# Dilated attention on tokens sorted by t mod 4, with a block's scores in one bank

## The chip, the cores and the metric

The kernel runs on one core of one Trainium2 chip. The metric is the device time of one execution in microseconds, as the median of several. Its engines are TensorE (PE, with PEld for its weight loads), VectorE (DVE), ScalarE (ACT), GpSimd (POOL) and SyncE (SP), which issues the DMAs. SBUF is the core's memory of 128 partitions; PSUM holds matmul results, in banks of 512 fp32 per partition.

## The reference

A trunk of two layers on 256 tokens of 2048 features. Layer A is a Mamba-2 mixer; then one set of keys and values is made from its output; layer B is attention in three groups of (window, dilation), eight heads of 128 features each. Every layer ends in a residual sum and a LayerNorm, and an adaLN (`silu(c) @ w + b`) gives shift, scale and gate.

```python
DIL_PATTERNS = ((128, 1), (512, 4), (2048, 16))

def _dilated_window_attention(q, k, v, window, dilation, slopes):
    """Causal dilated sliding window: query t attends t, t-d, ..., t-window."""
    s = jnp.einsum("brnqhe,brnkhe->brnhqk", qb, kb) * (E ** -0.5)
    ...
    alibi = -slopes[:, None, None] * (delta * dilation).astype(f32)[None]
    s = jnp.where(valid, s + alibi, -jnp.inf)
    ...

def reference(x, c, ...):
    for layer in range(DEPTH):
        shift, scale, gate = _adaln(c, ada_w[layer], ada_b[layer])
        h = x * (1.0 + scale) + shift
        y = _ssd_mixer(h, ...) if layer < N_A_LAYERS else _dilated_mixer(h, k_sh, v_sh, ...)
        x = _layer_norm(DEEPNORM_ALPHA * x + (1.0 + gate) * y, ln_g[layer], ln_b[layer])
        if layer == N_A_LAYERS - 1:
            k_sh, v_sh = _shared_kv(x, kv_w)
    return x
```

The outputs of the three groups are merged by their log-sum-exp, which is one softmax over the keys of all three groups together; a silu gate and the output projection follow. With 256 tokens, every key of a group with dilation d has the same t mod d as its query.

## The kernel before

All weights come from HBM once, in pieces of 128 x 1024 fp32 (512 KB, `raw`, six buffers, SP's queue). The products are made in reduced fp32 (fp32r) from halves: ACT writes the high half of a piece (`whi`, L94) and DVE the remainder (`wlo`, L95), with four buffers of each. PE then multiplies high by high, high by low and low by high (`cm_piece` L119 to L121, `tm_mults` L172 to L174); `cm_wide` (L151, L152) does high against both halves of x in one matmul of 512 columns and low against the high half in one of 256, 16 matmuls per piece.

The adaLN products are made on DVE: `ada_dot` (L236) multiplies a column block of 128 x 2048 (`araw`, 1 MB, two buffers) by the vector `cb_`, which lies in every partition, and sums. 96 such dots are dealt out between the weight pieces as background jobs.

After layer A's LayerNorm, `x_tiles` turns x over, 128 features at a time, 16 tiles: two PE transposes (L711), ACT writes scale times value plus bias as the high half (L714), DVE writes the same in full (`xtmp`, L715) and then the remainder (L716). Their results are the moving operand of the key, value and query projections (`xp`, which holds both halves). These tiles are made between the first pieces of the key projection. At the same time POOL applies the LayerNorm's weight and bias to the residual `u` (L766, L767).

Attention works on one of two query blocks of 128 tokens at a time. For query block b, the keys are those of block 0 to b, so a score matmul (L795) has 128 or 256 columns, three per block, one for each group, each in a PSUM tile of its own. DVE makes a group's bias from a table of distances and one of masks (L797, `bs`, loaded at L773), adds it to the scaled scores (L799), and takes the maximum over all groups (L801); ACT takes exp (L803); DVE normalises (L804, L805). The weights are transposed per group and key block (L809), copied from PSUM by ACT (L815) or, for the second group, DVE (L813), and multiplied with the values (L819, L820). DVE copies the result into `qq` (L821). `attend` does four heads per call and is called twice; after the queries, `z_gate` applies the gate, `split_act` (L195 on ACT, L196 on DVE) makes the halves `oghi` and `oglo`, and the output projection follows.

The order of all of this is not that of the code. A planner (`arrange`) takes the program's instructions, gives each a cost from a table, and, in some rounds of list scheduling, writes one fixed order per engine, which the chip then executes. Matmuls of a following projection are so put between those of attention. An edit at one place can move instructions anywhere.

Of the kernel before, what the change touches and what calls it, by code (L numbers as in the profile page):

```python
# [10 lines left out]
F32 = mybir.dt.float32  # L11
# [3 lines left out]
ALU = mybir.AluOpType  # L15
# [12 lines left out]
H = 8  # L28
# [18 lines left out]
CD, CA, NBIAS = 0, 256, 256 + 768  # L47
# [3 lines left out]
def trunk(ctx, tc, xT, x, c, par, cst, bias, lnrow, ada, wdt, win, wout, wkv, wk1, wbin, wbout, out):  # L51
# [655 lines left out]
    def x_tiles(q):  # L707
        for kt in (2 * q, 2 * q + 1):
            pt = aux.tile([P, 512], F32, name="aux")[:, :L]
            for b in range(2):  # L710
                T.transpose(pt[:, b * P:b * P + P], u[b][:, kt * P:kt * P + P], ident)  # L711
            t = pl.tile([P, L], F32, name="xtmp")
            g_, b_ = pv("lng")[:, kt:kt + 1], pv("lnb")[:, kt:kt + 1]
            S.activation(xhi[:, kt, :], pt, AF.Identity, bias=b_, scale=g_)  # L714
            V.tensor_scalar(t, pt, g_, b_, op0=ALU.mult, op1=ALU.add)  # L715
            V.tensor_tensor(xlo[:, kt, :], t, xhi[:, kt, :].bitcast(F32), op=ALU.subtract)  # L716
# [55 lines left out]
    bs = pc2.tile([P, NBIAS], F32, name="bs", bufs=1)  # L772
    nc.sync.dma_start(bs, bias)  # L773
    dmat = bs[:, CD:CD + 256]
    amask = bs[:, CA:CA + 768].rearrange("p (g k) -> p g k", g=3)
# [9 lines left out]
    def attend(hq, qq):  # L785

        for i in range(4):
            h = 4 * hq + i
            pT = pc2.tile([P, NG, 384], F32, name="pT", bufs=1)
            for b in range(2):  # L790
                n = P * (b + 1)
                sc = pc2.tile([P, NG, n], F32, name=f"sc{b}", bufs=1)
                for g in range(NG):
                    pq = aux.tile([P, 512], F32, name="aux")[:, :n]
                    T.matmul(pq, qq[:, g, i, b * P:b * P + P], kk[hq][:, g, i, :n], start=True, stop=True)  # L795
                    bi = pc2.tile([P, 256], F32, name="bi", bufs=2)[:, :n]
                    V.scalar_tensor_tensor(bi, dmat[:, 256 - n:], SLOPES[g * H + h], amask[:, g, 256 - n:],  # L797
                                           op0=ALU.mult, op1=ALU.add)
                    V.scalar_tensor_tensor(sc[:, g, :], pq, SCALE, bi, op0=ALU.mult, op1=ALU.add)  # L799
                nm = sm.tile([P, 1], F32, name="nm")  # L800
                V.tensor_reduce(nm, sc, axis=AX.XY, op=ALU.max, negate=True)  # L801
# [4 lines left out]
                for g in range(NG):  # L806
                    pp = aux2.tile([P, 512], F32, name="po")[:, :n]
                    for kb in range(b + 1):
                        T.transpose(pp[:, kb * P:kb * P + P], sc[:, g, kb * P:kb * P + P], ident)  # L809

                    d = pT[:, g, 0:P] if b == 0 else pT[:, g, P:384]
                    if g == 1:
                        V.tensor_copy(d, pp)  # L813
                    else:
                        S.activation(d, pp, AF.Copy)  # L815
            po = aux2.tile([P, 512], F32, name="po")[:, :L]
            v = vt[hq]
            for g in range(NG):
                T.matmul(po, v[:, g, 0, i * P:i * P + P], pT[:, g, 0:256], start=g == 0, stop=False)  # L819
                T.matmul(po[:, P:L], v[:, g, 1, i * P:i * P + P], pT[:, g, 256:384], start=False, stop=g == NG - 1)  # L820
# [534 lines left out]
def _layout(x, c, ada_w, ada_b, ln_g, ln_b, a_in_w, a_conv_w, a_conv_b, a_dt_bias,  # L1355
# [25 lines left out]
    delta = 128 + i[:, None] - np.arange(256)[None, :]  # L1381
    bias[:, CD:CD + 256] = -delta
    for g, (win_, dil) in enumerate(((128, 1), (512, 4), (2048, 16))):
        ok = (delta >= 0) & (delta % dil == 0) & (delta <= win_)
        bias[:, CA + 256 * g:CA + 256 * g + 256] = np.where(ok, 0.0, NEG)

# [35 lines left out]
```

## Time and profile before

| | us |
|---|---|
| median of 3 executions | 1284.6 (1283.5 to 1285.86) |
| profiled execution | 1281.55 |
| its span in the trace | 1279.8 |
| mean granted PE clock | 0.993 of full speed |
| x tiles | window 731 to 797 |
| first and second call of attention | windows 1069 to 1112 and 1157 to 1201 |

A row of instructions names its line, engine, operation and tiles, then count, total busy us, mean ns, and idle time of the engine ahead of them with what ended it. The chain of waits is the work that ended last, followed back from the end; its pieces have a start and a length in us. Matmuls are pipelined, so that a matmul's own mean length (393 ns for 512 columns, say) is more than the distance of two of them in the chain. A matmul of two fp32 operands (scores, PV) is recorded as two passes.

### The profile page before, as it was taken

How to read it: one execution, taken by the hardware profiler on the slowest of the kernel's cores; microseconds unless marked ns; L12 is line 12 of the kernel's file. 1: busy time of each engine (PE TensorE's matmuls, PEld its weight loads, DVE VectorE, ACT ScalarE, POOL GpSimd, SP SyncE). 2: the span in 40 equal slices, each digit the busy share in tenths (PEclk: the TensorE clock that was granted, in tenths of full speed). 3: DMA queues.
4: the chain of work that ended last, by engine and by line, in shares of the span. 5: the costliest groups of instructions: out<-in, count | busy, mean ns of one | idle time of the engine just before them, and what ended most of it. 6: DMA issues, size and time to landing. Idle time of an engine off the chain costs nothing.

```text
span 1279.8 us, 19378 instructions
## 1 busy us (share of the span) xinstructions
PE 1239.4 (97%) x7386; PEld 1095.2 (86%) x7386; DVE 1039.2 (81%) x1457; ACT 696.6 (54%) x1027; POOL 33.3 (3%) x20
## 2 busy tenths in 40 slices
PE   6999999999999999999999899999999999999995
PEld 4978999899899999788888699888888888888884
DVE  6999978999998887978895799998745647848778
ACT  4644566868577767764333444444445645444551
POOL 0000000000000000000000135000000000000000
PEclk9999999999999999999999899999999999999998
DMA  9999967887785556578997688999866663453571
GB/s 372 422 422 422 384 216 268 314 276 247 240 300 191 173 159 203 162 258 269 400 376 218 222 315 308 396 420 395 299 191 193 211 185 115 147 183 107 155 266 66
DMA packets 80449, 334.82 MB, mean 262 GB/s; under 512 B 9090, under 2 KB 9314, under 8 KB 67684
## 3 DMA queue, kind: packets, MB, share of 16 engines
q1 hardware_dynamic: 80356, 333.58, 73.5%
q8 instruction: 58, 0.95, 0.3%
q14 instruction: 35, 0.29, 0.1%
HBM read 331.37 MB, written 2.18 MB: 261 GB/s over the span
## 4 chain that ended last, share of the span: by engine, by line
PE 78%; DMA 12%; DVE 7%; ACT 1%; issue 1%; SPq 0%; DVEq 0%; ACTq 0%
PE acc L151 12%; PE acc L174 11%; PE acc L173 11%; PE acc L172 11%; PE acc L152 6%; DMA raw<-in_win 6%; PE acc L119 6%; PE acc L121 6%; PE acc L120 6%; DMA araw<-in_ada 5%; DVE wlo L95 2%; PE py L589 1%; DVE araw L236 1%; PE aux L795 1%; PE po L819 1%
## 5 line engine op out<-in xcount | busy, mean ns | idle before, releaser
L95 DVE TENSOR_TENSOR wlo<-raw,whi 128x1024 fp32r<-128x1024 f32 x395 | 488.9, 1244 | 176.5 <-ACT whi L94 175.2
L94 ACT ACTIVATE whi<-raw 128x1024 fp32r<-128x1024 f32 x395 | 417.1, 1057 | 382.1 <-PE acc L174 178.6
L119 PE MATMUL acc<-actT,whi 128*128 128x256 f32 x960 | 273.6, 288 | 11.8 <-ACT actT L382 7.4
L173 PE MATMUL acc<-wlo,actT 128*128 128x512 f32 x704 | 276.4, 393 | 0.6 <-DVE wlo L95 0.6
L172 PE MATMUL acc<-whi,actT 128*128 128x512 f32 x704 | 274.8, 393 | 1.6 <-ACT whi L94 1.0
L121 PE MATMUL acc<-actT,wlo 128*128 128x256 f32 x960 | 270.5, 285 | 1.4 <-DVE wlo L95 1.4
L120 PE MATMUL acc<-actT,whi 128*128 128x256 f32 x960 | 271.3, 285 | 0.0
L151 PE MATMUL acc<-actT,whi 128*128 128x512 f32 x704 | 251.3, 398 | 0.0
L236 DVE SCALAR_TENSOR_TENSOR araw<-araw,cb__72 128x2048 f32<-128x2048 f32 x96 | 218.4, 2286 | 9.0 <-DMA araw<-in_ada 5.7
L152 PE MATMUL acc<-actT,wlo 128*128 128x256 f32 x704 | 201.8, 287 | 0.6 <-DVE wlo L95 0.6
L119 PEld LDWEIGHTS acc<-actT,whi 128*128 128x128 f32 x960 | 185.2, 194 | 15.7 <-ACT actT L382 9.0
L121 PEld LDWEIGHTS acc<-actT,wlo 128*128 128x128 f32 x960 | 184.0, 193 | 2.3 <-DVE wlo L95 2.0
L120 PEld LDWEIGHTS acc<-actT,whi 128*128 128x128 f32 x960 | 185.1, 193 | 0.3
L174 PE MATMUL acc<-whi,actT 128*128 128x512 f32 x448 | 175.1, 391 | 0.0
L172 PEld LDWEIGHTS acc<-whi,actT 128*128 128x128 f32 x704 | 131.9, 188 | 30.1 <-ACT whi L94 2.8
L151 PEld LDWEIGHTS acc<-actT,whi 128*128 128x128 f32 x704 | 132.2, 188 | 29.2
L173 PEld LDWEIGHTS acc<-wlo,actT 128*128 128x128 f32 x704 | 132.3, 188 | 27.5 <-DVE wlo L95 1.1
L152 PEld LDWEIGHTS acc<-actT,wlo 128*128 128x128 f32 x704 | 133.0, 189 | 1.9 <-DVE wlo L95 1.2
L174 PE MATMUL acc<-whi,ylo 128*128 128x512 f32 x256 | 100.8, 394 | 0.0
L174 PEld LDWEIGHTS acc<-whi,actT 128*128 128x128 f32 x448 | 84.1, 188 | 17.5 <-issue 0.5
L174 PEld LDWEIGHTS acc<-whi,ylo 128*128 128x128 f32 x256 | 48.1, 188 | 9.4
L305 DVE SCALAR_TENSOR_TENSOR cacc<-acc,prm,cacc 128x255 f32<-128x255 f32 (+2 forms) x96 | 43.7, 475 | 2.7 <-ACT cacc L302 2.3
(205 smaller groups left out, 1083.1 us busy)
## 6 DMA issues: line engine op xcount, KB each, us to landing
araw<-in_ada SPq DMA_DIRECT2D x96, 1024.0 KB, 7.2
raw<-in_win SPq DMA_DIRECT2D x160, 512.0 KB, 4.9
raw<-in_wkv SPq DMA_DIRECT2D x72, 512.0 KB, 4.9
raw<-in_wout SPq DMA_DIRECT2D x64, 512.0 KB, 5.6
raw<-in_wbin SPq DMA_DIRECT2D x64, 512.0 KB, 4.0
raw<-in_wk SPq DMA_DIRECT2D x24, 512.0 KB, 6.6
cbc<-cumd SPq DMA_DIRECT2D x16, 512.0 KB, 5.3
raw<-in_wbout SPq DMA_DIRECT2D x16, 512.0 KB, 4.3
```

The costliest lines, as they stand in the source:

```text
L94: S.activation(hi, raw, AF.Copy)
L95: V.tensor_tensor(lo, raw, hi.bitcast(F32), op=ALU.subtract)
L119: T.matmul(o, hi[:, k, c_], ahi[:, kt, :], start=first, stop=False, skip_group_check=True)
L120: T.matmul(o, hi[:, k, c_], alo[:, kt, :], start=False, stop=False, skip_group_check=True)
L121: T.matmul(o, lo[:, k, c_], ahi[:, kt, :], start=False, stop=kt == k1 - 1, skip_group_check=True)
L151: T.matmul(ps[n], hi[:, k, c_], xp[:, kt], start=kt == 0, stop=False, skip_group_check=True)
L152: T.matmul(ps[n][:, 0, :], lo[:, k, c_], xhi[:, kt, :], start=False, stop=kt == KT - 1, skip_group_check=True)
L172: T.matmul(ps[b], h_, hi[:, k, :], start=kt == k0, stop=False)
L173: T.matmul(ps[b], h_, lo[:, k, :], start=False, stop=False)
L174: T.matmul(ps[b], l_, hi[:, k, :], start=False, stop=kt == k1 - 1)
L236: V.scalar_tensor_tensor(raw, raw, 1.0, cb_, op0=ALU.mult, op1=ALU.mult, accum_out=mod[layer][:, ct, j:j + 1])
L305: V.scalar_tensor_tensor(acc[:, o:], ps[:, :L - o], w[:, j:j + 1], acc[:, o:], op0=ALU.mult, op1=ALU.add)
```

## The change

Layer B works on its tokens in the order 0, 4, 8, ..., 1, 5, 9, ..., 2, ..., 3, ... . Block 0 then holds the tokens with t mod 4 of 0 and 1, block 1 the others, and the groups of dilation 4 and 16 need only keys of the query's own block. Dilation 1 needs both blocks, whichever the query block. For each query block there are 128 + 128 + 256 = 512 scores, which fill one PSUM bank.

```diff
             pt = aux.tile([P, 512], F32, name="aux")[:, :L]
             for b in range(2):
                 T.transpose(pt[:, b * P:b * P + P], u[b][:, kt * P:kt * P + P], ident)
+            pt = pt.rearrange("p (j r) -> p r j", r=4)
...
-            S.activation(xhi[:, kt, :], pt, AF.Identity, bias=b_, scale=g_)
-            V.tensor_scalar(t, pt, g_, b_, op0=ALU.mult, op1=ALU.add)
+            S.activation(xhi[:, kt, :].rearrange("p (r j) -> p r j", r=4), pt, AF.Identity, bias=b_, scale=g_)
+            V.tensor_scalar(t.rearrange("p (r j) -> p r j", r=4), pt, g_, b_, op0=ALU.mult, op1=ALU.add)
...
-    bs = pc2.tile([P, NBIAS], F32, name="bs", bufs=1)
+    bs = cb_[:, :NBIAS]
     nc.sync.dma_start(bs, bias)
-    dmat = bs[:, CD:CD + 256]
-    amask = bs[:, CA:CA + 768].rearrange("p (g k) -> p g k", g=3)
+    dmat, amask = bs[:, CD:CD + NKEY], bs[:, CA:CA + NKEY]
...
+            bi = pc2.tile([P, NKEY], F32, name="bi", bufs=2)
+            for g, c in ((1, slice(0, P)), (2, slice(P, 2 * P)), (0, slice(2 * P, NKEY))):
+                V.scalar_tensor_tensor(bi[:, c], dmat[:, c], SLOPES[g * H + h], amask[:, c], op0=ALU.mult, op1=ALU.add)
+            bi = bi.rearrange("p (a k) -> p a k", a=3)
+            pT = pc2.tile([P, 2, 4, P], F32, name="pT", bufs=1)
             for b in range(2):
...
+                cb = slice(b * P, b * P + P)
+                pq = aux.tile([P, 512], F32, name="aux")
+                for g in (1, 2):
+                    T.matmul(pq[:, (g - 1) * P:g * P], qq[:, g, i, cb], kk[hq][:, g, i, cb], start=True, stop=True)
+                T.matmul(pq[:, 2 * P:], qq[:, 0, i, cb], kk[hq][:, 0, i, :], start=True, stop=True)
+                sc = pc2.tile([P, 512], F32, name=f"sc{b}", bufs=1)
+                V.scalar_tensor_tensor(sc.rearrange("p (a k) -> p a k", a=2), pq.rearrange("p (a k) -> p a k", a=2), SCALE,
+                                       bi[:, 0:b + 2:b + 1], op0=ALU.mult, op1=ALU.add)
...
+                pp = aux2.tile([P, 512], F32, name="po")
+                for k in range(4):
+                    T.transpose(pp[:, k * P:k * P + P], sc[:, k * P:k * P + P], ident)
+                if b == 0:
+                    V.tensor_copy(pT[:, b].rearrange("p k q -> p (k q)"), pp)
+                else:
+                    S.activation(pT[:, b].rearrange("p k q -> p (k q)"), pp, AF.Copy)
...
+            T.matmul(po, v[:, 0, 0, ci], pT[:, :, 2, :], start=True, stop=False)
+            T.matmul(po, v[:, 0, 1, ci], pT[:, :, 3, :], start=False, stop=False)
+            for b in range(2):
+                for g in (1, 2):
+                    T.matmul(po[:, b * P:b * P + P], v[:, g, b, ci], pT[:, b, g - 1, :], start=False, stop=b == 1 and g == 2)
             V.tensor_copy(qq[:, 0, i, :], po)
...
-        split_act(oghi[:, c, :], oglo[:, c, :], qs[hq][:, 0])
+        hi, lo = (t[:, c, :].rearrange("p i (j r) -> p i j r", r=4) for t in (oghi, oglo))
+        for i in range(4):
+            split_act(hi[:, i], lo[:, i], qs[hq][:, 0, i].rearrange("p (r j) -> p j r", r=4))
```

The sorting is done where the x tiles are read from PSUM, and undone where the attention output is split. The bias table, of three times 256 columns for distances and the same for masks (768 KB, before 512 KB), lies in `cb_`, the vector that the dots read. The tables themselves are made on the host in the new order. The high and low halves of the attention output are written in the order of the code before. Line numbers after L95 move by one or more: L95, L236, L715 and L716 are L96, L237, L717 and L718; scores are L799 and L800, the scaled add L802, the transposes L812, PV L819, L820 and L823.

The planner writes a new order for the whole program. The first place is DVE in the stretch of the x tiles, some rows in. `wlo` is the low half of a weight piece, `araw` the dot with `cb_`, `xtmp` and `actT` the x tile. Before:

```order
L95 TENSOR_TENSOR wlo<-raw,whi 128x1024
L236 SCALAR_TENSOR_TENSOR araw,mod_83<-araw,cb__72 128x2048
L715 TENSOR_SCALAR xtmp<-aux,prm 128x256 x2
L716 TENSOR_TENSOR actT<-xtmp,actT 128x256
L95 TENSOR_TENSOR wlo<-raw,whi 128x1024
L716 TENSOR_TENSOR actT<-xtmp,actT 128x256
L95 TENSOR_TENSOR wlo<-raw,whi 128x1024
L236 SCALAR_TENSOR_TENSOR araw,mod_83<-araw,cb__72 128x2048
L95 TENSOR_TENSOR wlo<-raw,whi 128x1024
L715 TENSOR_SCALAR xtmp<-aux,prm 128x256 x2
```

and of the changed program, from the same weight split on:

```order
L96 TENSOR_TENSOR wlo<-raw,whi 128x1024
L237 SCALAR_TENSOR_TENSOR araw,mod_83<-araw,cb__72 128x2048
L96 TENSOR_TENSOR wlo<-raw,whi 128x1024
L237 SCALAR_TENSOR_TENSOR araw,mod_83<-araw,cb__72 128x2048
L717 TENSOR_SCALAR xtmp<-aux,prm 128x256 x2
L718 TENSOR_TENSOR actT<-xtmp,actT 128x256
L96 TENSOR_TENSOR wlo<-raw,whi 128x1024
L718 TENSOR_TENSOR actT<-xtmp,actT 128x256
L96 TENSOR_TENSOR wlo<-raw,whi 128x1024 x2
L237 SCALAR_TENSOR_TENSOR araw,mod_83<-araw,cb__72 128x2048
```

A second dot stands ahead of the third pair of x tiles. Up to the last x tile there are ten dots from here on, where there were eight.

The second place is PE in the first call of attention, around the first head's PV. `acc` is the projection that fills, `aux` scores, `po` transposed weights and PV. Before:

```order
L795 MATMUL aux<-kk_7193,qq 128x256
L809 MATMUL po<-cc,sc_10321 128x128 x2
L151 MATMUL acc<-actT,whi 128x512
L152 MATMUL acc<-actT,wlo 128x256
L819 MATMUL po<-pT,vt_7195 128x256
L820 MATMUL po<-pT,vt_7195 128x128
L819 MATMUL po<-pT,vt_7195 128x256
L820 MATMUL po<-pT,vt_7195 128x128
L819 MATMUL po<-pT,vt_7195 128x256
L820 MATMUL po<-pT,vt_7195 128x128
L795 MATMUL aux<-kk_7193,qq 128x256 x2
```

and of the changed program:

```order
L152 MATMUL acc<-actT,whi 128x512
L799 MATMUL aux<-kk_7193,qq 128x128 x2
L819 MATMUL po<-pT,vt_7195 128x256
L820 MATMUL po<-pT,vt_7195 128x256
L823 MATMUL po<-pT,vt_7195 128x128 x4
L800 MATMUL aux<-kk_7193,qq 128x256
L799 MATMUL aux<-kk_7193,qq 128x128 x2
L800 MATMUL aux<-kk_7193,qq 128x256
L153 MATMUL acc<-actT,wlo 128x256
L812 MATMUL po<-cc,sc_10346 128x128 x4
```

The scores of a later head stand around the PV of the first one in both. Between the first score and the last PV of a call PE's order holds 123 and 132 filling matmuls before (first and second call), and 72 and 72 in the changed program. All dots come earlier, as the bias is loaded into `cb_` behind the last of them.

More of the change, by code (lines that the diff above doesn't have):

```diff
@@ L45 @@
 CI, CT, CM, NCONST = 0, 128, 256, 512
-CD, CA, NBIAS = 0, 256, 256 + 768
+NKEY = 768
+CD, CA, NBIAS = 0, NKEY, 2 * NKEY
 @with_exitstack
@@ L1380, in _layout @@
     bias = np.zeros((P, NBIAS), f)
[L1381 to L1385, printed above, removed]
+    at = np.arange(L).reshape(64, 4).T.reshape(-1)
+    delta = at[:, None] - at[None, :]
+    near = delta[:P, :P]
+    delta = np.concatenate([near, near, delta[:P], delta[P:]], 1)
+    win_, dil = (np.repeat(a, (P, P, 2 * L))[None, :] for a in ((512, 2048, 128), (4, 16, 1)))
+    bias[:, CD:CD + NKEY] = -delta
+    bias[:, CA:CA + NKEY] = np.where((delta >= 0) & (delta % dil == 0) & (delta <= win_), 0.0, NEG)
     ada = ada_w.reshape(2, D, 3, KT, P).transpose(0, 2, 3, 4, 1)
```

26 lines of the change are left out of this document (2 added, 24 removed).

## The prediction

> **What bounds the kernel now.** I read three views first: the page's busy times and its chain by engine, then the table of windows, then the chain of waits in the two stretches that the change touches.
>
> ```profile
> span 1279.8 us, 19378 instructions
> PE 1239.4 (97%) x7386; PEld 1095.2 (86%) x7386; DVE 1039.2 (81%) x1457; ACT 696.6 (54%) x1027; POOL 33.3 (3%) x20
> PE 78%; DMA 12%; DVE 7%; ACT 1%; issue 1%; SPq 0%; DVEq 0%; ACTq 0%
> ```
>
> The chain is PE for 78%. But 97% busy is a mean over stages; what the change is worth is settled in the stages where it acts, so the windows come next (columns: length, then busy us and instructions of PE, PEld, DVE, ACT, POOL, then granted clock, DMA share, GB/s).
>
> ```profile
> 0.00:150.00 150.00, 133.78 (x821) 116.88 (x822) 129.58 (x141) 74.69 (x101) 0.20 (x4) 1.00 1.00 410
> ...
> 731.00:797.00 66.00, 65.47 (x542) 65.05 (x542) 65.70 (x65) 28.24 (x35) 33.08 (x16) 0.99 0.85 310
> 830.00:1069.00 239.00, 239.00 (x1196) 202.56 (x1196) 161.70 (x179) 115.80 (x149) 0.00 (x0) 1.00 0.78 267
> 1069.00:1112.00 43.00, 43.00 (x266) 38.43 (x266) 39.42 (x97) 22.15 (x47) 0.00 (x0) 1.00 0.31 94
> 1157.00:1201.00 44.00, 44.00 (x273) 39.22 (x272) 40.10 (x98) 24.18 (x50) 0.00 (x0) 1.00 0.36 109
> 1201.00:1260.00 59.00, 59.00 (x290) 49.76 (x290) 43.29 (x61) 25.45 (x30) 0.00 (x0) 1.00 0.54 187
> ```
>
> The two attention calls are the windows at 1069 and 1157. There PE is never idle, and DVE is at 92% and 91% (39.42 of 43, 40.10 of 44). So in attention a matmul removed is time removed, and a DVE or ACT instruction removed is worth nothing by itself. The window 731 to 797, in which x is turned over into tiles of features by tokens, is the opposite case: DVE 65.70 of 66, with no room at all. Up to 797 PE just keeps pace (65.47), and then the chain of waits passes through DVE:
>
> ```profile
> 792.42 2.25 DVE wlo L95
> 794.72 0.39 PE acc L121
> ```
>
> and PE's own waits between 731 and 830 are few and short:
>
> ```profile
> PE acc L152 <- DVE wlo L95: 0.6, 2, 0.4
> PE acc L121 <- DVE wlo L95: 0.5, 1, 0.5
> ```
>
> So PE and DVE are balanced to within 1.1 us there: the piece of weights that PE needs next arrives from DVE when PE has just run out.
>
> **PE's work in attention.** Scores, transposes and PV as the chain has them (L795 and L819/L820 are recorded as two passes per instruction):
>
> ```profile
> 1157.19 0.44 PE aux L795 x4
> 1157.63 0.23 PE acc L151
> 1159.21 0.12 PE acc L152
> 1159.56 0.43 PE aux L795 x2
> 1165.90 0.44 PE po L809 x4
> 1168.26 0.43 PE po L819 x2
> 1168.69 0.22 PE po L820 x2
> ```
>
> A 128-column score costs 0.44 / 2 = 0.22 us, a 256-column one 0.43, a transpose 0.44 / 4 = 0.11, and PV 0.43 and 0.22 for the same widths. A head had three scores of each width, and has four narrow and two wide: 1.95 becomes 1.74, so -0.21. PV goes from three and three to two wide and four narrow, again -0.21. Transposes go from nine to eight, -0.11. That is -0.53 a head and, over 8 heads, **-4.2 us**. Nothing hides this gain: PE is busy in all 43 and 44 us of both windows, and stays so until 1260. The bounds are -4.2 and, if PE then waits for softmax as often as it is spared work, 0.
>
> **DVE's and ACT's work in attention.** For these I need the costs of one instruction against its length:
>
> ```profile
> L799 DVE SCALAR_TENSOR_TENSOR sc<-aux,bi 128x256 f32<-128x256 f32 x24 | 10.0, 420 | 0.7
> L799 DVE SCALAR_TENSOR_TENSOR sc<-aux,bi 128x128 f32<-128x128 f32 x24 | 6.5, 287 | 2.8 <-PE aux L795 2.0 <-PE po L809 0.6
> L801 DVE TENSOR_REDUCE nm<-sc 128x1 f32<-128x768 f32 x8 | 7.6, 950 | 0.2
> L801 DVE TENSOR_REDUCE nm<-sc 128x1 f32<-128x384 f32 x8 | 4.4, 546 | 0.1
> L805 DVE TENSOR_SCALAR sc<-sc,den 128x768 f32<-128x768 f32 x8 | 4.9, 618 | 0.2
> L805 DVE TENSOR_SCALAR sc<-sc,den 128x384 f32<-128x384 f32 x8 | 3.3, 418 | 0.2
> L803 ACT ACTIVATE sc<-sc,nm 128x768 f32<-128x768 f32 x8 | 7.5, 932 | 3.4 <-DVE nm L801 3.3
> L803 ACT ACTIVATE sc<-sc,nm 128x384 f32<-128x384 f32 x8 | 4.9, 613 | 7.0 <-DVE nm L801 7.0
> L803 ACT ACTIVATION_READ_ACCUMULATOR sc<-sc,nm 128x1 f32 x16 | 3.0, 186 | 0.0
> L804 DVE RECIPROCAL den<-den 128x1 f32<-128x1 f32 x8 | 1.3, 162 | 0.4
> L95 DVE TENSOR_TENSOR wlo<-raw,whi 128x1024 fp32r<-128x1024 f32 x395 | 488.9, 1244 | 176.5 <-ACT whi L94 175.2
> ```
>
> The two L799 rows give 133 ns per 128 columns, so 0.69 us at 512; between the other pairs, 512 columns are 0.68 (maximum), 0.49 (normalise) and 0.72 (exp). Scaled add: 3 x 0.287 + 3 x 0.420 = 2.12 becomes 2 x 0.69 = 1.38. The bias is made once a head instead of per block: 2.12 becomes 0.29 + 0.29 + 0.69 = 1.27. Maximum 1.50 becomes 1.36, normalise 1.04 becomes 0.98, copies of the transposed weights, at L799's prices, 0.71 become 0.69. Together 7.5 become 5.7, -1.8 us of DVE a head, and ACT has less too (one copy of 512 columns in place of four). PE is what ends these windows, so I count **0**. The gain is not kept as slack either, as the order shows: between the first score and the last PV of a call PE's order holds 72 matmuls of the following projection as filling, in both calls, where it held 123 and 132. With PE's 4.36 us of its own a head (1.74 + 1.74 + 8 x 0.11) and 18 fillers, alternately 0.23 and 0.12 us apart, 4.36 + 9 x 0.35 = 7.5 us of PE stand against 7.8 us of DVE rows (the 5.7, 0.42 for PV's copy, 0.3 of reciprocals, and 18/16 of a weight split of 1.24, since 16 fillers use one up). The same sum for before is 7.5 + 0.42 + 0.3 + 2 x 1.24 = 10.7 us, where the window says 39.42 / 4 = 9.9, since neighbouring rows overlap; scaled by that, 7.8 is 7.2, or 96% of PE's time instead of 92%. Bounds: 0 (everything covered) and +1.0 a head, since the second block's way from score to PV is 0.69 + 0.68 + 0.72 + 0.19 + 0.16 + 0.49 + 0.44 + 0.69 = 4.1 plus the first block's 1.86 of DVE, 5.9 us, against a cover of 1.74 + 3.15 = 4.9. The next head's transposes and PV also stand in between, so I am near the lower end: **+0.5** in all.
>
> **The stretch from 731 to 830.** The bias now lies in the buffer that the adaLN dots read, so its DMA cannot go before the last dot, and the order has all dots earlier. In the stretch of the x tiles it has ten dots where it had eight; both orders have had 64 when it starts. DVE's rows there:
>
> ```profile
> L95 DVE TENSOR_TENSOR wlo<-raw,whi 128x1024 fp32r<-128x1024 f32 x20 | 33.1, 1654 | 0.0
> L236 DVE SCALAR_TENSOR_TENSOR araw<-araw,cb__72 128x2048 f32<-128x2048 f32 x8 | 18.2, 2280 | 0.0
> L715 DVE TENSOR_SCALAR xtmp<-aux,prm 128x256 f32<-128x256 f32 x14 | 7.0, 536 | 0.7 <-ACT actT L714 0.6
> ```
>
> The weight splits take 1654 ns in the mean while POOL works (2.25 in the chain above), more than the 1.24 us over the whole run, so DVE cannot make up for anything. Two dots more are 2 x 2.2 = 4.4 us of DVE in a stretch where DVE has 0.3 us free and PE has no reserve, and PE then waits as long. They are missing later, after 830, where DVE is busy 161.70 of 239 us and their absence earns nothing. Of the 4.4 I take off 0.5: the 1.1 us of waits above come partly from this same shortage, and a PE that is late no longer meets them. **+3.9**, bounds 0 (PE lives on splits that were made ahead) and 4.4.
>
> **The x tiles' reads.** ACT's L714 and DVE's L715 now read PSUM with a step of 16 bytes, 16 times each, and write in order. No instruction of the trace reads PSUM with a step. The nearest are additions in SBUF with a step of 12 bytes (x2), against short ones (x16):
>
> ```profile
> L714 ACT ACTIVATE actT<-aux,prm 128x256 fp32r<-128x256 f32 x16 | 8.0, 551 | 0.3 <-PE aux L711 0.3
> L241 DVE TENSOR_TENSOR mod<-mod,adab 128x2 f32<-128x2 f32 x16 | 2.4, 156 | 0.1
> L241 DVE TENSOR_TENSOR mod<-mod,adab 128x16 f32<-128x16 f32 x2 | 0.3, 174 | 0.0
> ```
>
> 14 elements more cost 18 ns, 1.3 ns each, hardly above the 1.04 of L799 (133 / 128): no second cycle. So I take **0**, with +4.3 as the other end (256 x 1.04 ns more for each of the 16 on DVE; ACT's 16 lie in its 38 idle us). [...]
>
> **What is hidden or small.** The last dot and the bias load before:
>
> ```profile
> 914.35 2.29 DVE L236 SCALAR_TENSOR_TENSOR araw<-araw,cb__72 128x2048 f32<-128x2048 f32 x1
> 1006.61 0.33 SPq L773 DMA_DIRECT2D bs<-in_bias  x1
> ```
>
> 92 us lie between the two, so a wait of the bias DMA for the last dot costs nothing, nor do 256 KB more. The attention output is split in 8 pieces of 256 columns instead of 2 of 1024, read with a step of 256 bytes: per four heads, by the slopes above, 0.5 for ACT's first piece and 4 x 0.42 on DVE, 2.2 us, against 1.1 on ACT and then 1.2 on DVE before, so ready no later, and PE is busy throughout 1201 to 1260; **0**, with +1 if the step costs. The order also swaps a few rows and loads in the first 150 us, where DMA is full (share 1.00); there a 1 MB or 512 KB load moved by one place shifts work by at most its own time, 2.6 us at 410 GB/s, either way and mostly back again: I take 0, with -1 to +1.
>
> **Sum** on the profiled execution (1281.55 us for a span of 1279.8): -4.2 + 3.9 + 0.5 = +0.2, so 1281.75. That execution lies 3.05 below the median of 1284.6, so the forecast is **1284.8**.
>
> **The rivals.** B: the two dots cost nothing. For it: only 1.1 us of waits between 731 and 830, and four buffers of splits. Against: DVE without idle time for 66 us. It leaves out the 3.9: 1280.9. C, on the slower side: PSUM with a step goes at half rate, and the full DVE passes it on. It decides as soon as L715's successor is above 0.56 us, since DVE has 0.3 us free for 16 of them; at 0.27 us more each it is +4.3, 1289.1. For it: no reading of PSUM in this trace speaks against it. Against: the SBUF rows. D: with fewer fillers PE waits for softmax. It decides from where a block's way to PV exceeds what stands in between; at half of the 1.0 us a head found above, 8 x 0.5 = 4.0 in place of 0.5, 1288.3. For it: DVE at 96%. Against: the fillers can be prepared early, and PE had no wait there at 92%.
>
> **Chances.** My forecast A 0.50, B 0.23, C 0.13, D 0.14. A difference of 0.2% (2.6 us) is about what a measurement tells from none: faster is below 1282.0, slower above 1287.2. A's own range is 1282 to 1287.5, with its unknowns (±1 at the start, 0 to +1 at the splits, 0 to 4.4 for the dots): faster 0.12, same 0.27, slower 0.11. B: 0.19, 0.04, 0. C: 0, 0.01, 0.12. D: 0, 0.03, 0.11. Together faster 0.31, same 0.35, slower 0.34. The range, 1279.5 to 1290, reaches past B and C by about a microsecond each.
>
> **What would show it.** In the profile of the changed kernel: attention windows shorter by 51 to 60 fillers and by 2.1 us more each, with PE still without idle time (A, B; not D, where PE's waits there name L802 or a copy); between 731 and 830 PE waits for the weight split of some 4 us in place of 1.1 (A) or not (B); the x tiles' DVE row at 0.54 (A, B) or about 0.8 us (C). I would be wrong altogether if the stretch 150 to 731, whose order hardly differs, changed its length, or if PE lost time behind the bias DMA.

## The result, and the profile after

| | before | changed |
|---|---|---|
| median of 20 executions, us | 1285.01 (1283.36 to 1291.98) | 1289.56 (1285.78 to 1292.2) |
| profiled execution, us | 1281.55 | 1289.36 |
| its span, us | 1279.8 | 1287.5 |
| mean granted PE clock | 0.993 | 0.990 |

The ratio is 1.0027, with a 95% interval of [1.0016, 1.0037]: the change costs 2 to 5 us, 3.5 in the middle. The forecast was 1284.8, no difference that can be told, in a range of 1279.5 to 1290. The time lies near the range's upper end and above the 1282 to 1287.5 that the forecast gave for its own mechanism; the sign is that of the slower rivals. One kernel's executions scatter by 6 to 9 us. The two profiled ones are 7.8 us apart, more than the medians, and the one of before, 1281.55, lies below all 20 executions of the table, so a difference of the two traces is too large by some 3 us. Below, the traces tell the mechanism and the ratios the size. Ratios are turned into microseconds with some 1285.5 us for the kernel before.

The page of the changed kernel, busy times and the chain by engine:

```profile
span 1287.5 us, 19278 instructions
PE 1240.0 (96%) x7378; PEld 1093.5 (85%) x7378; DVE 1031.9 (80%) x1399; ACT 694.9 (54%) x1009; POOL 34.0 (3%) x20
PE 76%; DMA 14%; DVE 7%; issue 1%; ACT 1%; SPq 0%; DVEq 0%; ACTq 0%
```

PE is busy as long as before (1240.0 us against 1239.4) in a span 7.7 us longer, so it waits more, and the chain has more DMA. Where, is seen by the start of the same instruction in both. First the changed kernel's timeline of PE (start, length, what, and the idle time ahead with its releaser):

```profile
732.25 0.69 PE L712 MATMUL aux<-cc,u 128*128 128x128 f32 x2 [5.73 <-ACT u L697]
1082.40 0.39 PE L799 MATMUL aux<-kk,qq 128*128 128x128 f32 x2
1229.36 0.40 PE L173 MATMUL acc<-whi,kk 128*128 128x512 f32 x1
```

and the same three of the kernel before, the first x tile, the first score, and the first matmul of the output projection:

```profile
726.73 0.48 PE L711 MATMUL aux<-cc,u 128*128 128x128 f32 x1 [5.73 <-ACT u L696]
1069.66 0.50 PE L795 MATMUL aux<-kk,qq 128*128 128x128 f32 x3
1221.39 0.39 PE L172 MATMUL acc<-whi,kk 128*128 128x512 f32 x1
```

| stretch | before | changed | difference |
|---|---|---|---|
| start to first x tile (layer A) | 726.73 | 732.25 | +5.5 |
| first x tile to first score | 342.93 | 350.15 | +7.2 |
| first score to output projection (attention) | 151.73 | 146.96 | -4.8 |
| output projection to the end of the span | 58.4 | 58.1 | -0.3 |

So in this pair of traces attention gained what it should, the x tiles lost more than the forecast had, and layer A, whose instructions the change doesn't touch, lost 5.5 us. Layer A's waits sit at one place. PE's timeline there, in the changed kernel:

```profile
233.09 0.73 PE L173 MATMUL acc<-whi,actT 128*128 128x512 f32 x2 [2.13 <-ACT whi L95]
234.20 0.66 PE L560 MATMUL aux<-cc,xs 128*128 128x128 f32 x4 [0.37 <-ACT cb L539]
236.25 1.12 PE L590 MATMUL py<-xd,seg 128*128 128x64 f32 x4 [1.40 <-DVE xd L562]
```

and in the kernel before:

```profile
232.84 1.46 PE L589 MATMUL py<-xd,seg 128*128 128x64 f32 x9 [0.46 <-DVE xd L561]
```

PE waits 3.9 us in three pieces where it waited 0.7 (0.46 here and 0.19 at 235.26). The clock falls as well. This is the window 223 to 247 of the kernel before, then of the changed one (the sixth of the plain figures from the left, after POOL, is the granted clock):

```profile
223.00:247.00 24.00, 23.33 (x128) 19.61 (x127) 21.93 (x31) 20.01 (x33) 0.00 (x0) 1.00 0.93 355
```

```profile
223.00:247.00 24.00, 20.10 (x99) 16.36 (x98) 17.82 (x24) 17.82 (x38) 0.00 (x0) 0.86 0.84 323
```

In windows of 0.5 us the clock of the changed kernel is 1.00 from 223 to 235 us and from 242 to 247, and 0.50 between 235.5 and 241.5. The mean of 0.86 over 24 us is then 2 x 0.14 x 24 = 6.7 us at half speed, and PE does 99 matmuls instead of 128. If PE had work for all of this time, that cost up to 3.4 us by estimate; with the 3.2 us of longer waits this is more than the 5.5, so how the loss divides between the two is not settled. What was late is in the chain of waits of the changed kernel, in order of time:

```profile
213.20 7.58 DMA cumd<-araw
220.81 0.33 SPq L544
221.70 7.43 DMA araw<-in_ada
229.26 2.30 DVE araw L237 x2
231.56 0.35 DVE cb L538
232.00 1.23 DVE seg L552
233.23 2.36 DVE cacc L306 x6
235.59 0.61 DVE xd L562
```

`cumd` is a small tensor that goes to HBM and comes back in every partition (`cbc`, L544). SP's new order issues a dot's 1 MB load directly ahead of the write and two weight loads behind it; the write takes 7.58 us, and SP stands on L544 until it has landed. The next dot's load starts only then, and that dot stands in DVE's queue ahead of the products that PE needs. ACT is late by the same write: it waits 5.70 us for `cbc` (0.98 us before), and the high half that PE waits for longest, 2.13 us, is made behind that. ACT's timeline in the changed kernel:

```profile
225.36 3.33 ACT L549 ACTIVATE seg<-cbc,cumT 128x128 f32<-128x128 f32 x11 [5.70 <-DMA cbc<-cumd]
```

Between the x tiles and the first score PE waits for weight splits (waits of PE, 728 to 825 us: in total, times, longest), and DVE's rows in the same window are these:

```profile
PE acc L122 <- DVE wlo L96: 2.9, 4, 1.0
PE acc L153 <- DVE wlo L96: 1.1, 1, 1.1
PE aux L712 <- DVE xtmp L717: 0.9, 1, 0.9
```

```profile
L96 DVE TENSOR_TENSOR wlo<-raw,whi 128x1024 fp32r<-128x1024 f32 x27 | 38.0, 1417 | 0.0
L237 DVE SCALAR_TENSOR_TENSOR araw<-araw,cb__72 128x2048 f32<-128x2048 f32 x14 | 36.2, 2583 | 2.1 <-DMA araw<-in_ada 2.0
L718 DVE TENSOR_TENSOR actT<-xtmp,actT 128x256 fp32r<-128x256 f32 x16 | 10.2, 641 | 0.1
L717 DVE TENSOR_SCALAR xtmp<-aux,prm 128x256 f32<-128x256 f32 x16 | 8.0, 536 | 0.6 <-ACT actT L716 0.6
```

and ACT's row for the same tiles, over the whole run:

```profile
L716 ACT ACTIVATE actT<-aux,prm 128x256 fp32r<-128x256 f32 x16 | 8.1, 554 | 0.7 <-PE aux L712 0.7
```

The waits for splits are 4.0 us where the kernel before had 1.1, and one of 0.9 us for an x tile comes on top. In the same window of the kernel before the dots took 2282 ns and the splits 1508: the dots have become longer and the splits shorter. The stepped reads (L717 with 536 ns against 536, L716 with 554 against 551) cost nothing.

In attention PE has no idle time in either kernel: from the first score to the output projection it is busy 151.73 of 151.73 us before, and 146.96 of 146.96 in the changed kernel. The rows of 512 columns measured what the forecast had read off between the shorter ones:

```profile
L802 DVE SCALAR_TENSOR_TENSOR sc<-aux,bi 128x512 f32<-128x512 f32 x16 | 10.9, 686 | 1.6 <-PE aux L800 1.2 <-PE po L812 0.3
L805 DVE TENSOR_REDUCE nm<-sc 128x1 f32<-128x512 f32 x16 | 10.6, 677 | 0.1
L809 DVE TENSOR_SCALAR sc<-sc,den 128x512 f32<-128x512 f32 x16 | 7.6, 482 | 0.3
L807 ACT ACTIVATE sc<-sc,nm 128x512 f32<-128x512 f32 x16 | 11.4, 715 | 7.5 <-DVE nm L805 7.5
```

(0.69, 0.68, 0.49 and 0.72 us had been worked out.) The split of the attention output, in the changed kernel:

```profile
L196 ACT ACTIVATE kk<-qq 128x256 fp32r<-128x256 f32 x8 | 4.8, 663 | 0.3 <-DVE qq L831 0.3
L197 DVE TENSOR_TENSOR vt<-qq,kk 128x256 fp32r<-128x256 f32 x8 | 4.7, 628 | 0.3 <-ACT kk L196 0.3
```

256 columns should have taken DVE 0.42 us.

### The profile page after: what moved, and what is told of

It is laid out like the page before. It is cut to its first block, busy times and chain, and to the rows that moved or that the text cites. A ratio compares the mean times of both kernels' runs of the same rounds, so it can differ in the third digit from the quotient of the medians.

```text
span 1287.5 us, 19278 instructions
## 1 busy us (share of the span) xinstructions
PE 1240.0 (96%) x7378; PEld 1093.5 (85%) x7378; DVE 1031.9 (80%) x1399; ACT 694.9 (54%) x1009; POOL 34.0 (3%) x20
## 3 DMA queue, kind: packets, MB, share of 16 engines
HBM read 331.63 MB, written 2.18 MB: 259 GB/s over the span
## 4 chain that ended last, share of the span: by engine, by line
PE 76%; DMA 14%; DVE 7%; issue 1%; ACT 1%; SPq 0%; DVEq 0%; ACTq 0%
PE acc L152 12%; PE acc L175 11%; PE acc L174 11%; PE acc L173 11%; PE acc L153 6%; DMA raw<-in_win 6%; DMA araw<-in_ada 6%; PE acc L120 6%; PE acc L122 6%; PE acc L121 6%; PE py L590 2%; DVE wlo L96 2%; DVE araw L237 1%; DMA prm<-in_par 1%; DVE seg L552 1%
## 5 line engine op out<-in xcount | busy, mean ns | idle before, releaser
L96 DVE TENSOR_TENSOR wlo<-raw,whi 128x1024 fp32r<-128x1024 f32 x395 | 485.5, 1236 | 188.7 <-ACT whi L95 186.7
L95 ACT ACTIVATE whi<-raw 128x1024 fp32r<-128x1024 f32 x395 | 417.1, 1057 | 383.1 <-PE acc L175 177.7
L237 DVE SCALAR_TENSOR_TENSOR araw<-araw,cb__72 128x2048 f32<-128x2048 f32 x96 | 222.7, 2329 | 16.5 <-DMA araw<-in_ada 12.8
L549 ACT ACTIVATE seg<-cbc,cumT 128x128 f32<-128x128 f32 x128 | 40.2, 388 | 13.0 <-PE py L590 7.2
```

The lines of the kernel that those rows point to most:

```text
L95: S.activation(hi, raw, AF.Copy)
L96: V.tensor_tensor(lo, raw, hi.bitcast(F32), op=ALU.subtract)
L237: V.scalar_tensor_tensor(raw, raw, 1.0, cb_, op0=ALU.mult, op1=ALU.mult, accum_out=mod[layer][:, ct, j:j + 1])
L549: S.activation(seg[:, hh, b, :], cbc[:, hh, b, :], AF.Relu, bias=cumT[:, b, h0 + hh:h0 + hh + 1], scale=-1.0)
```

## The experiments

All instructions up to the bias load are the same in both programs, and both orders have done the same set of them when the first `xtmp` is made. So one program can be given the other's order for a part. "Layer A" is that common set; "up to the last dot" is what either order has done when its last adaLN dot is made, with the x tiles in it. A list `HEAD` of instruction numbers, written out in the kernel, takes the place of the planner's order:

```diff
+    mine = set(HEAD)
+    best = best[0], HEAD + [i for i in best[1] if i not in mine]
     last = {}
     for i in best[1]:
```

### The changed program, layer A in the order before

> The changed program, but all instructions up to the first xtmp stand in the order of the kernel before (they are the same instructions in both). Theory T: the profiled loss of 5.5 us ahead of the x tiles is the new order's, by the loads and the cumd write on SP near 213 us. Then the first transpose of the x tiles falls back from 732.3 to about 726.7 us, the clock stays whole near 235 us, and the time is 4 to 6 us under the changed kernel's, 1284 to 1286. Rival R: that loss is chance of one execution (a clock that fell), and the order costs nothing. Then the time stays within 1.5 us of the changed kernel's 1289.6.

Measured: 1284.43 us, ratio to before 0.9988 [0.9975, 1.0001]. Against the change's 1.0027 that is 5.0 us less (3 to 7 by the two intervals). The first x tile starts at 726.42 us, and the window 223 to 247 has its full clock again:

```profile
223.00:247.00 24.00, 23.03 (x124) 19.20 (x123) 21.96 (x31) 19.75 (x33) 0.00 (x0) 1.00 0.91 350
```

PE's longest gap there is 0.76 us. The theory holds: the order, not chance, cost layer A its time. The granted clocks of all executions say the same: with the old order of layer A, 106 of 171 had a mean of 0.991 or more, with the changed or a mixed order 1 of 68. Some executions with the old order lose clock too, then; where in them no trace shows.

### The changed program, everything up to the last dot in the order before

> The changed program with everything up to the last adaLN dot in the order of the kernel before; attention, the reads of PSUM with a step and the split of the attention output are those of the change. Theory T: the x tiles lose 7.2 us by the order alone (dots and their loads earlier), and what is left of the change is attention's gain of 4.8 us. Then it takes 4 to 5 us less than the kernel before, about 1280, and PE waits for weight splits between 731 and 830 us for about 1 us. Rival S: the stretch of the x tiles loses by the stepped reads or by something else of the change; then it keeps at least half of the 7.2 us and the time is 1284 or more.

Measured: 1278.68 us, ratio 0.9952 [0.9933, 0.9971], -6.2 us, **faster than both kernels**. From the first x tile to the first score it takes 343.71 us (342.93 before), so the stepped reads and the bias in `cb_` are not what lost time there. PE's waits there:

```profile
PE acc L153 <- DVE wlo L96: 0.9, 2, 0.7
PE acc L122 <- DVE wlo L96: 0.5, 1, 0.5
```

Its attention takes 4.8 us less than that of before in the trace, as in the changed kernel; the ratio's interval (-8.6 to -3.7 us) holds that number.

### The kernel before, layer A in the changed order

> The kernel before, with all instructions up to the first xtmp in the changed program's order, and nothing else of the change. Theory T: it loses what the changed kernel lost there, 4 to 6 us: 1289 to 1291 against 1285, first transpose of the x tiles near 732 us, PE waiting some 2 us for a high half near 231 us. Rival R (chance): within 1.5 us of the kernel before.

Measured: 1290.16 us, ratio 1.0037 [1.0022, 1.0052], +4.8 us. The first x tile starts at 731.88 us, with PE gaps of 0.72, 0.37 and 2.03 us near 232 to 236 and a clock of 0.86 in the window 223 to 247. The long wait fell on the product (L561) and not on a high half, otherwise as expected. Nothing of the change is in this kernel but the order of layer A. Even so its trace loses time behind layer A too: from the first x tile to the first score it takes 346.80 us, +3.9, with the rows of the x tiles, and the eight dots among them, as before. PE's waits there:

```profile
PE acc L121 <- DVE wlo L95: 2.8, 2, 2.4
PE acc L152 <- DVE wlo L95: 0.7, 1, 0.7
```

So one trace of this stretch can be some 4 us longer, with 3.5 us of waits for splits, without any dot moved.

### The kernel before, from the first x tile to the last dot in the changed order

> The kernel before, with the instructions from the first xtmp to the last adaLN dot in the changed program's order, so with ten dots in the stretch of the x tiles in place of eight; the x tiles read PSUM without a step, and attention and the bias tile are as before. Theory T: it loses about 7 us, 1291 to 1293 against 1285. Rival S (the stepped reads or other parts of the change cost it): under 3 us of loss.

Measured: 1289.63 us, ratio 1.0032 [1.002, 1.0044], +4.1 us [2.6, 5.7]; less than expected, and far from nothing. First x tile to first score: 349.10 us in the trace, +6.2. Over all traces without a further edit of the stretch it took 342.9 to 346.8 us with the old order of the x tiles (four kernels) and 349.0 to 351.3 with the changed one (five). Together the three pieces make 4.8 + 4.1 - 6.2 = +2.7 us, against 3.5 [2, 5] measured for the change.

### Layer A again: only the loads around the `cumd` write

Of layer A's changed order, 17 rows of SP go back (rows 116 to 132 of its queue: the `cbc` loads stand right behind the write again, and the dot's load behind them). A second kernel has 16 rows of DVE put back as well.

```diff
+seq["SP"][116:133] = before["SP"][116:133]
+seq["DVE"][178:194] = before["DVE"][178:194]    # the second kernel only
```

> The changed program in its own order, except for 17 rows of SP's queue around the cumd write near 213 us, which stand as in the kernel before: one 1 MB load of araw and two weight loads move from ahead of the cbc loads to behind them. Every other engine keeps the changed order. Theory T1: these rows are the whole loss ahead of the x tiles; then the first transpose is at 726 to 728 us and the time at 1284 to 1286, as with the whole of layer A in the old order. Rival: the order of DVE, ACT or PE in layer A takes part; then the first transpose stays 2 us or more behind 726.7 us.

Measured: 1288.39 us, ratio 1.0012 [0.9997, 1.0027], -1.9 us against the change, which is not clear of the noise; the first x tile starts at 733.47 us. The rival holds. The write is now quick, ACT's wait for `cbc` is 0.42 us, and the wait has moved to a dot, which stands ahead of where its load can be ready. Chain of waits of this kernel, and DVE's timeline:

```profile
213.57 2.18 DMA cumd<-araw
216.63 7.24 DMA araw<-in_ada
```

```profile
223.96 2.29 DVE L237 SCALAR_TENSOR_TENSOR araw<-araw,cb__72 128x2048 f32<-128x2048 f32 x1 [5.87 <-DMA araw<-in_ada]
```

> The changed program in its own order, except for the 17 rows of SP's queue as in the run that brought the cumd write forward, and 16 rows of DVE's queue there, three dots among them, which stand behind a weight split (one also behind the product that the cumd write sends) as in the kernel before. Theory L: the loss ahead of the x tiles is dots that stand in DVE's queue ahead of their loads' landing; the loads alone did not mend it because a dot then waited 5.9 us. With both, DVE's wait for araw there is under 2 us, the first transpose is at 726 to 728.5 us, the time 1283.5 to 1286. Rival: the order of ACT or PE there has a part; then the first transpose stays behind 729 us.

Measured: 1288.93 us, ratio 1.0018 [1.0001, 1.0035]; the first x tile at 732.75 us. DVE's waits for `araw` between 200 and 237 us fell to 4.7 us (8.1 in the changed kernel, 7.2 with the loads alone, 1.1 before), PE's gap is one of 2.59 us, and the clock still falls (0.79 in the window). Neither the theory's number nor its time came. Ahead of the gap its chain of waits still has the write, 4.55 us here, and behind it a dot's load of 10.11 us. The part that these rows have in the loss is not told apart from the others'.

### The x tiles: DVE's time, the loads, or POOL

The first three kernels start from the kernel before with the changed order from the first x tile to the last dot (+4.1 us), the fourth from the changed kernel. In the first, two of the ten dots multiply 64 columns:

```diff
+        n = 64 if dots.append(0) or len(dots) - 1 in (65, 68) else D
+        V.scalar_tensor_tensor(raw[:, :n], raw[:, :n], 1.0, cb_[:, :n], op0=ALU.mult, op1=ALU.mult,
```

> The kernel before with the changed order from the first xtmp to the last dot, whole (ten dots in the stretch of the x tiles), but two of these ten dots multiply 64 columns in place of 2048; their 1 MB loads stay. It leaves out most of the sum in those two. Theory D: the loss of 4 to 6 us comes from DVE's time for the two dots, 2 x 2.2 us. Then the time is within 1.5 us of the kernel before, and PE's waits for weight splits between 731 and 830 us are about 1 us. Rival M: it comes from the earlier 1 MB loads that crowd out the weight loads; then the loss stays at 3 us or more.

Measured: 1289.7 us, ratio 1.0028 [1.0014, 1.0042], +3.6 us. The rival's number, though not by crowding: the next dot waits instead. DVE's timeline:

```profile
759.93 2.28 DVE L239 SCALAR_TENSOR_TENSOR araw<-araw,cb__72 128x2048 f32<-128x2048 f32 x1
763.28 0.21 DVE L239 SCALAR_TENSOR_TENSOR araw<-araw,cb__72 128x64 f32<-128x64 f32 x1
769.50 2.29 DVE L239 SCALAR_TENSOR_TENSOR araw<-araw,cb__72 128x2048 f32<-128x2048 f32 x1 [2.15 <-DMA araw<-in_ada]
```

The third dot's load needs the buffer of the first, which ends at 762.2; it lands 7.2 us later, whatever the second dot takes. DVE's waits for `araw` rose from 3.4 to 5.3 us.

In the second kernel POOL's additions work on 8 columns:

```diff
-                PO.tensor_tensor(u[b][:, cs_], u[b][:, cs_], lnr[0], op=ALU.mult)
-                PO.tensor_tensor(u[b][:, cs_], u[b][:, cs_], lnr[1], op=ALU.add)
+                c1_ = slice(512 * n, 512 * n + 8)
+                PO.tensor_tensor(u[b][:, c1_], u[b][:, c1_], lnr[0][:, :8], op=ALU.mult)
+                PO.tensor_tensor(u[b][:, c1_], u[b][:, c1_], lnr[1][:, :8], op=ALU.add)
```

> The kernel before with the changed order from the first xtmp to the last dot (ten whole dots), but POOL's 16 instructions on the residual work on 8 columns in place of 512, which leaves most of the LayerNorm's weight and bias out of the residual. Theory D: DVE is the bound of the stretch and POOL's work slows its weight splits from 1.22 to 1.65 us; without it DVE has some 8 us more, the two dots fit, and the time is at or up to 2 us below the kernel before. Rival M (loads): the loss of 3 us or more stays.

Measured: 1285.65 us, ratio 0.9995 [0.998, 1.001]: the loss is gone, with the same ten dots and loads. From the first x tile to the first score it takes 342.85 us. DVE's groups between 731 and 797 us, first in the kernel that this one starts from, then here:

```profile
L95 DVE TENSOR_TENSOR wlo<-raw,whi 128x1024 fp32r<-128x1024 f32 x19 | 27.3, 1446 | 0.0
L236 DVE SCALAR_TENSOR_TENSOR araw<-araw,cb__72 128x2048 f32<-128x2048 f32 x10 | 25.4, 2537 | 0.6 <-DMA araw<-in_ada 0.6
```

```profile
L236 DVE SCALAR_TENSOR_TENSOR araw<-araw,cb__72 128x2048 f32<-128x2048 f32 x12 | 27.5, 2290 | 1.5 <-DMA araw<-in_ada 1.5
L95 DVE TENSOR_TENSOR wlo<-raw,whi 128x1024 fp32r<-128x1024 f32 x21 | 25.5, 1217 | 2.6 <-ACT whi L94 2.5
```

A split takes 1217 ns, not 1446, and a dot 2290, not 2537. PE waits for no split in this stretch. Crowded loads as the cause by themselves (rival M) fall with it; DVE's waits for `araw`, 3.8 us between 727 and 840, are as long as with POOL's whole work (3.4). No run has the short additions in the order before, so what POOL costs that order is not known.

The third kernel has three buffers for the dots' loads:

```diff
-        raw = pool.tile([P, D], F32, name="araw", bufs=2)
+        raw = pool.tile([P, D], F32, name="araw", bufs=3 if pool.name == "pl" else 2)
```

> The kernel before with the changed order from the first xtmp to the last dot (the run that lost 4.1 us), but with three buffers for the 1 MB loads of the dots there in place of two. Theory L, formed after the run with two short dots kept its loss: a dot that stands earlier in DVE's queue waits for its own load, which can only start when the dot two before it has freed its buffer and takes 7 us to land; the weight split behind it waits too, and POOL's slowing of DVE leaves no time to make up for it. With a third buffer the loads start earlier: DVE's waits for araw fall from 3.4 to under 1.5 us, and at least half of the loss goes, 1285 to 1287.5 against 1285.5 of before. Rival W: the loads are late because DMA is full or SP's queue stands still for other reasons; then the waits stay at 3 us and the loss at 3 us or more.

Measured: 1287.28 us, ratio 1.0019 [1.0, 1.0038], +2.4 us. DVE's waits for `araw` are down to 0.2 us as expected, and the time is less by 1.7 us in the middle, within the time that was expected but short of half the loss, and the intervals overlap: whether the buffer helps is not shown. PE still waits 1.8 us for one split:

```profile
PE acc L121 <- DVE wlo L95: 1.8, 1, 1.8
```

The fourth is the changed kernel with the same three buffers:

> The changed kernel in its own order, with three buffers in place of two for the dots' loads from the x tiles on. Theory L: of its 7.2 us between the first transpose and the first score, half or more goes (3 to 6 us), so 1284 to 1287 in all, since the loss in layer A stays. Rival W (DMA full): it stays within 1.5 us of the changed kernel's 1289.6.

Measured: 1288.59 us, ratio 1.0022 [1.0006, 1.0037]; -0.6 us against the change, not to be told from nothing. The third buffer is no repair of the changed kernel.

### Both at once, and more rows of layer A

The order of the change up to the last dot in the kernel before, with two short dots and three buffers, and 53 rows of DVE with the 17 of SP put back in layer A.

> The kernel before with the changed order up to the last dot, and two separate edits. In layer A, 17 rows of SP's queue and 53 of DVE's around the cumd write stand as before (ACT and PE keep the changed order). From the x tiles on there are three araw buffers, and two of the ten dots multiply 64 columns in place of 2048, which leaves most of the sum out of those two. Layer A, theory L: with DVE's and SP's rows the PE gap near 232 us is under 1 us as before (with 16 DVE rows it was 2.6), the clock does not fall, and the first transpose is at 726 to 728 us; rival (ACT or PE rows, or the fall of the clock comes anyhow): behind 730 us. X tiles, theory B (both at once: DVE's 4.4 us for two more dots, and the waits of dots for loads that took their place when the dots were short): without either, first transpose to first score takes within 1.5 us of the 342.9 us of the kernel before (5 to 6 us more with either edit alone was 4.5 and 6.4); rival: 4 us more or longer, and then something else holds it. Time with both right: 1284 to 1287.

Measured: 1294.72 us, ratio 1.0068 [1.0045, 1.0092], the slowest of all. Layer A became worse by the mixture: the first x tile starts at 737.6 us, PE has gaps of 1.68 us at 212 us and of 1.01, 2.09 and 0.74 us later, and the clock in the window 223 to 247 is 0.79. So these rows of DVE and SP, put back without those of ACT and PE, do not mend it. From the first x tile to the first score it takes 346.97 us, +4.0 on the kernel before. DVE waits 3.3 us for `araw` all the same. The expected end of the loss did not come, but the reading is weak: the trace with layer A's changed order alone has +3.9 in this stretch.

### How the split of the attention output is written

The kernel that was fastest, with the halves read in order and written with a step of 16 bytes, in place of read with a step of 256 bytes and written in order.

```diff
-        hi, lo = (t[:, c, :].rearrange("p i (j r) -> p i j r", r=4) for t in (oghi, oglo))
+        hi, lo = (t[:, c, :].rearrange("p i (j r) -> p i r j", r=4) for t in (oghi, oglo))
...
-            split_act(hi[:, i], lo[:, i], qs[hq][:, 0, i].rearrange("p (r j) -> p j r", r=4))
+            split_act(hi[:, i], lo[:, i], qs[hq][:, 0, i].rearrange("p (r j) -> p r j", r=4))
```

> The changed program with everything up to the last dot in the order of the kernel before (as in the run before that took 1278.7), and the halves of the attention output are read in order and written with a step of 16 bytes, in place of read with a step of 256 bytes and written in order. If the step of 256 bytes makes the reads slow (0.63 us on DVE for 256 columns, where 0.42 is paid in order), the two rows of the split fall to about 0.42 on DVE and 0.40 on ACT; if any step in SBUF costs, they stay. As PE is not idle there, the time stays within 1 us of that run.

Measured: 1279.0 us, ratio 0.9954 [0.9937, 0.997], as in that run, which this confirms. DVE's and ACT's rows stay:

```profile
L197 DVE TENSOR_TENSOR vt<-qq,kk 128x256 fp32r<-128x256 f32 x8 | 4.6, 644 | 0.3 <-ACT kk L196 0.3
L196 ACT ACTIVATE kk<-qq 128x256 fp32r<-128x256 f32 x8 | 4.3, 676 | 0.3 <-DVE qq L831 0.3
```

## Why the prediction was right and wrong

- **What bounds each stage:** right. Attention is PE's, the x tiles are DVE's, and the forecast's windows said so.
- **Attention, -4.2 + 0.5:** right. The first pair of traces has -4.8 us; over seven traces of the old attention (150.9 to 152.3 us) and seven of the new (146.9 to 148.0) the means differ by -4.1. PE never waited for softmax (rival D), with 72 fillers in place of 123 and 132. DVE's lighter load is worth nothing, as forecast.
- **The x tiles, +3.9:** the size was right (+4.1 [2.6, 5.7] by the run with that order alone; 7.2 in the one trace of the changed kernel). The working was not. It multiplied two dots by their 2.2 us. With the two made short, the loss stayed; with POOL out of the way and both dots whole, it went. The sign that the forecast had set for it, some 4 us of waits for splits in place of 1.1, came with 4.0, but it does not single out the dots: the trace with layer A's order alone has 3.5 us with no dot moved. What the runs show is that the changed order of this stretch costs 4.1 us, and nothing once POOL's work is out of the way. That a dot moved forward is paid for either by its length or by a dot's wait for its load fits the two short dots, but is not shown: with three buffers as well the loss did not end, and with POOL's work short the waits for loads stayed and cost nothing. Rival B's time is out, since the stretch does lose; which rows lose it is open.
- **Stepped reads of PSUM, 0:** right; rival C is out. ACT's row is 554 ns (551 before), DVE's 536 (536). The half rate that C supposed, and the 4.3 us worked out for it from this case's rows, show in no run.
- **Split of the attention output, 0:** right for the time (the end from the output projection on is no longer), but the rows are 0.63 us and not 0.42; PE covered it.
- **Bias load, 0:** right; in the changed kernel it starts at 918.5 us, the first row that reads it at 1020.3, and none of DVE's waits between 900 and 1230 us is for it.
- **The order of the start, 0 with -1 to +1:** this is the step that failed. The forecast looked at the first 150 us and at the two stretches with changed code, and said of the stretch from 150 to 731 that its order "hardly differs". It bounded the effect of a moved load by the load's own 2.6 us. The runs show +4.8 and -5.0 us for layer A's order, put in and taken out. In the trace PE waits 3.9 us where it waited 0.7, behind a write that took 7.58 us, and the clock is halved for 6.7 us; neither is bounded by one load's time. It had listed a changed length of just this stretch as what would prove it wrong.

The sum, with this term at 4.8 in place of 0, is 1284.8 + 4.8 = 1289.6; it was 1289.56. That the others fit so closely is in part luck, as the intervals are 2 to 5 us wide. Luck, too, is that the range held the time: it reached up to 1290 for rivals C and D, and neither took part. What stays open: which rows of layer A do it. Taking back SP's 17, or those with 16 or 53 of DVE's, did not mend it; taking back all did.

## What to carry to other kernels

Where a planner writes the order of the whole program, a local change must be read in the order everywhere, above all at round trips through HBM (here the `cumd` write, 7.58 us in the changed kernel and 2.18 with the loads around it put back) and at big loads that a queue in fixed order waits for (a dot's, 7.43 and 7.24 us in the same two): a gain of 4 to 5 us in one stage was given back, and more, by the order in two others. Freezing the old order up to the change and planning only what follows kept the gain here, 1278.7 us. And where an engine has no idle time, look for what slows it from outside (here POOL: a split took 1446 ns with its additions whole, 1217 with short ones) ahead of counting what it is given.

## What the runs showed of the hardware

**Short waits of PE near each other went with a fall of the clock.** In the thin stretch near 232 us, the traces of eight kernels (the one before, and the seven with its order of layer A) had gaps of PE of 0.8 us or less in a piece and at most 1.2 in all, and a full clock in the window 223 to 247. The six with the changed or a mixed order had 2.5 to 3.9 us in all, and 0.74 to 0.86 of the clock, 6.7 to 12.5 us at half speed by the same sum as above. No single gap there was longer than 2.6 us. The gap of 5.73 us ahead of the first x tile went with one as well: in the 6 us behind it the clock was 0.57 in the kernel before and 0.61 in the changed one. Near 232 us no gap was that long; there it fell with waits that have small matmuls between them. How the two are joined is not shown.

**256 columns with a step took longer in SBUF than others in order; in PSUM they did not.** 256 columns in SBUF took DVE 628 ns when read with a step of 256 bytes and 644 when written with one of 16; ACT took 663 and 676. The same two lines of the changed kernel, on another tile and in order, took 419 and 403:

```profile
L197 DVE TENSOR_TENSOR actT<-htmp,actT 128x256 fp32r<-128x256 f32 x16 | 6.4, 419 | 1.9 <-ACT actT L196 1.9
L196 ACT ACTIVATE actT<-htmp 128x256 fp32r<-128x256 f32 x16 | 5.9, 403 | 0.6 <-PE acc L174 0.6
```

From PSUM with a step of 16 bytes both engines were as fast as in order (536 and 554 ns against 536 and 551). The forecast had taken sums of 16 elements in SBUF, 1.3 ns each, as its measure for both; they were too short to tell.

**POOL's additions lengthen DVE's dots as well,** from 2.29 to 2.54 us in the mean between 731 and 797 us, besides its splits, from 1.22 to 1.45 (the runs with short and with whole additions, in the same order).
